# Two-by-two steps for four pairs of up-projection blocks and for one more pair of down-projection rows, in a one-core transformer block

## The chip, the cores and the metric

The kernel runs on one core of a Trainium2 chip. The metric is the device time of one launch in microseconds (us), taken as the median over runs. The core has five engines, each with its own list of instructions that it works through in order: TensorE (PE, matmuls, with weight loads shown apart as PEld), VectorE (DVE), ScalarE (ACT), GpSimd (POOL) and SyncE (SP). SP and POOL also issue most of the transfers (DMAs), from a hardware queue (q1 in the profile, issued by SP) and a software queue (q0, issued by POOL). POOL's DMAs can add to what lies at the destination; the kernel uses them to add weights up in DRAM.

## The reference

One layer of a gated block, batch 1, 512 tokens, width 1024, in float32:

```
h = rms_norm(x);  proj = h @ w_in          # conv B | C | in | q | k | v | f | gates
y_conv = (B * causal_dwconv(C * in)) @ w_out_conv
y_attn = attention(q, k, v, log sigmoid f) @ w_out_attn
x = x + (sigmoid(g_conv) * y_conv + sigmoid(g_attn) * y_attn) @ w_o
h = rms_norm(x)
up = causal_dwconv(h @ w_up)               # 1024 -> 2 * 2816, three taps a channel
a, b = split(up)
x = x + (silu(a) * b) @ w_down             # 2816 -> 1024
return rms_norm(x)
```

The change touches `h @ w_up`, `@ w_down` and what lies between and behind them.

## The kernel before

Activations lie with channels on the 128 partitions and the 512 tokens in the free dimension. Every matmul is 128x128 by 128x256. To keep float32 accuracy each operand is split into a high and a low part of a shorter format; a product is then three matmuls: high by high, low weight by high, high weight by low (`mm3` and `passes`, matmuls of L277 and L295).

**The weights' way.** `stream` lists all weight chunks in the order of use (512 KB for a block of 128 output channels). `load` (L201) brings a chunk to one of five `raw` buffers by an SP DMA; `split` (L244, L248) makes the high part on ACT (`wh_...`) and the low part on DVE (`wl_...`), in two buffers each, so the split of chunk k waits until the matmuls of chunk k-2 are done, and the load of chunk k for the split of chunk k-5. A chunk's matmuls take all products by `wh` first where `passes` orders them so, then those by `wl`. Work that may wait (`later`) is handed out behind the splits.

**Two by two steps.** Where a pair of output blocks by a pair of input blocks is needed, the kernel can do a 2x2 step with 7 products instead of 8 (table `PROD`): each product is of a sum of weights by a sum of activations, and the results are combined afterwards. `double(n)` puts two chunks in the stream for such a step: `P{n}` (768 columns, three plain products, `wst`) and `F{n}` (1024 columns, the four sums of weights). The sums are made in DRAM: `group` yields six operations for each group of two steps, three SP copies (L131) and three adding POOL DMAs (L134), each of which needs the one before; they are issued one at a time by `tick()`, in lockstep for three groups. Ticks come once for a unit of the attention and once for some chunks' splits.

**The stages**, with their time in the profile: attention with the input projections (to about 182 us); the gates, six pairs as 2x2 steps of 84 matmuls, with the mixing products (182 to 295); `wo`, eight blocks (295 to 338), whose evacuation makes x1 = x + p, its scaled high and low parts x1h and x1l, and its squares; the up blocks of phase 0, pairs j = 0 to 11 of two blocks (a and b) of 48 matmuls each (338 to 471); down, phase 0, 12 steps of 42 matmuls (L295 `dn`, 471 to 528); up, phase 1, ten pairs (to 637); down, phase 1, five steps of 42 matmuls for rows 0, 1, 4, 5 of the output (to 660); rows 2 and 3 plainly (`pd`, 120 matmuls, to 674); rows 6 and 7 plainly in two halves of the tokens (`pdA`, `pdB`); then the final norm, the products by it (L1204) and the stores.

**A pair of up blocks.** `up` (L976) multiplies each result by the norm's row (`fz`, from PSUM into SBUF), then takes three taps (L569 on ACT, L570 and L573 on DVE). `glu` makes silu(a) times b (L986 on ACT, L989 and L996 on POOL) and, after every second pair, the sums of the products for the 2x2 steps of down (L1006 to L1011) and their high and low parts (L1015 on ACT, L1016 on DVE).

**The end of down.** `combine` (L1042 to L1061) recombines a finished pair of rows, `final_square` (L1073 to L1078) adds its squares to `ssq3` and scales it. `fin_sum` (L1185 to L1188) and `fin_col` (L1193) do rows 6 and 7; `pc_n` (L336) sums the squares over the partitions on PE and releases the final products and stores of a half of the tokens.

A scheduler (Tile) orders the instructions on each engine by data and priorities, save those that `keep` pins.

Of the kernel before, what the change touches and what calls it, by code (L numbers as in the profile page):

```python
# [59 lines left out]
def block_kernel(ctx, tc, xT, vecs, wv, win, wmix, wo, wup, wst, wdp, outT):  # L60
# [57 lines left out]
    groups += [list(range(n, min(n + 2, NFF))) for n in range(0, NFF, 2)]  # L118
    todo = []

    def group(i):
# [6 lines left out]
        w, f = ((lambda a, b, z=z: z[:, :, a * P : b * P]) for z in (w, t))  # L128
# [16 lines left out]
    for i0, i1 in ((0, ngate), (ngate, len(groups))):  # L145
        for i in range(i0, i1, 3):
            todo += [op for ops in zip(*(group(x) for x in range(i, min(i + 3, i1)))) for op in ops]
# [5 lines left out]
    def double(n):  # L153
        return [(f"P{n}", wst[n, :, : 6 * P], 6 * P), (f"F{n}", sums[n], D)]
# [15 lines left out]
    for ph, (j0, j1) in enumerate(PHASES):  # L170
        stream += [(f"up{j}", wup[j], D) for j in range(2 * j0, 2 * j1)]
        for _ in STEPS[ph]:
            stream += double(n)
            n += 1
# [48 lines left out]
    def split(hl=None):  # L223
# [6 lines left out]
        if k >= gs0 and (nm[0] in "imwu" or nm[0] == "F" and int(nm[1:]) % 2):  # L230
            tick()
        if hl is None:
# [21 lines left out]
        run_later(k, {"u": 1.7, "P": 1.6, "F": 0.75}.get(nm[0], 3.5))  # L254
# [53 lines left out]
    def place_of(f, s_):  # L308
        c = 2 * (f % 3 if f < 6 else 3) + s_
# [140 lines left out]
    for kb in range(KB):  # L450
# [345 lines left out]
    def mt(name):  # L796
        return mp.tile([P, S], F32, tag="mt", name=name, bufs=5)
# [89 lines left out]
    x1 = xp.tile([P, KB, S], F32, tag="x1", name="x1")  # L887
# [50 lines left out]
    for j in range(KB):  # L938
# [3 lines left out]
        xr = mt(f"xr{j}")  # L942
        nc.gpsimd.dma_start(xr, xT[:, j, :])
        nc.vector.tensor_add(x1[:, j, :], p, xr)
        nc.scalar.activation(x1h[:, j, :], x1[:, j, :], AF.Copy, scale=col(G2 + j))
# [381 lines left out]
```

## Time and profile before

| what | value |
|---|---|
| median of 3 runs | 701.1 us (700.32 to 701.42) |
| the profiled execution's time | 700.69 us |
| its span | 698.9 us |
| around the span | 1.8 us |
| PE busy | 690.2 us (99%) |
| DVE, ACT, POOL busy | 498.3 (71%), 341.8 (49%), 156.4 (22%) us |
| granted clock of TensorE, mean | 0.996 |
| moved by DMA | 115.31 MB, mean 165 GB/s |

A row of groups names the line and engine, the operation with what it writes and reads, the count, the busy time and the mean of one in ns, then the idle time ahead of it and who ended it. A matmul's own duration overlaps its neighbours' (a row has 276 ns, but 504 of them take 57.12 us), so the time of a run of matmuls is read from the chain of waits, where a run of matmuls stands as one piece with its start, its length and its count.

### The profile page before, as it was taken

What the parts mean: (1) busy time and instruction counts of PE and PEld (TensorE: products, weight loads), DVE (VectorE), ACT (ScalarE), POOL (GpSimd) and SP (SyncE); (2) the same over time, 40 slices, a digit from 0 to 9 for tenths busy, and PEclk for the clock granted to TensorE, in tenths of its full rate; (3) what the DMA queues carried; (4) which work ended last, traced back from release to release, by engine and by line L of the source; (5) the groups of instructions that cost most, each with busy time, mean ns of one, the idle gap of its engine ahead of it and who ended that gap; (6) DMA issues with size and microseconds to landing.
All of it is one profiled execution on the core that took longest, in us unless ns stands there. A gap on an engine that the chain in (4) does not pass through costs nothing.

```text
span 698.9 us, 14573 instructions
## 1 busy us (share of the span) xinstructions
PE 690.2 (99%) x6005; PEld 688.1 (98%) x6005; DVE 498.3 (71%) x797; ACT 341.8 (49%) x541; POOL 156.4 (22%) x176
## 2 busy tenths in 40 slices
PE   9999999999999999999999999999999999999996
PEld 8999999999999999999999999999999999999995
DVE  6677777786687787754377777778774677877853
ACT  6665656655664433543345443455443345444542
POOL 5125645434011001035321212230000211100002
PEclk9999999999999999999999999999999999999998
DMA  8627877467379777658556637577675433224503
GB/s 308 201 74 209 200 158 200 118 163 179 92 176 268 232 212 214 225 183 207 140 133 197 170 106 199 141 171 206 191 222 177 116 118 92 84 84 133 177 1 121
DMA packets 51538, 115.31 MB, mean 165 GB/s; under 512 B 4720, under 2 KB 22256, under 8 KB 51472
## 3 DMA queue, kind: packets, MB, share of 16 engines
q1 hardware_dynamic: 36880, 93.73, 41.4%
q0 software_dynamic: 13328, 19.44, 17.5%
q10 hardware_dynamic: 1264, 1.22, 0.5%
q8 instruction: 47, 0.77, 0.4%
q14 instruction: 19, 0.16, 0.1%
HBM read 112.20 MB, written 32.51 MB: 207 GB/s over the span
## 4 chain that ended last, share of the span: by engine, by line
PE 92%; DVE 2%; ACT 2%; issue 1%; DMA 1%; ACTq 0%; SPq 0%; POOL 0%; DVEq 0%
PE p_up L277 26%; PE p_in L277 14%; PE dn L295 12%; PE p_up L295 8%; PE gs L295 8%; PE p_wo L277 6%; PE yc L295 3%; PE ya L277 3%; PE pd L277 2%; PE o L659 2%; PE pa L478 2%; PE pb L480 1%; PE tp L644 1%; PE pdB L277 1%; PE pdA L277 1%
## 5 line engine op out<-in xcount | busy, mean ns | idle before, releaser
L277 PE MATMUL p_up<-x1h,wh_up 128*128 128x256 f32 x536 | 104.5, 276 | 0.0
L277 PE MATMUL p_up<-x1l,wh_up 128*128 128x256 f32 x536 | 104.4, 276 | 0.0
L277 PE MATMUL p_up<-x1h,wl_up 128*128 128x256 f32 x536 | 104.3, 276 | 0.0
L244 ACT ACTIVATE wh_up<-raw_up 128x1024 fp32r<-128x1024 f32 x44 | 46.7, 1061 | 89.2 <-PE p_up L277 75.7
L277 PEld LDWEIGHTS p_up<-x1h,wh_up 128*128 128x128 f32 x536 | 80.8, 188 | 0.0
L277 PEld LDWEIGHTS p_up<-x1l,wh_up 128*128 128x128 f32 x536 | 80.7, 188 | 0.0
L277 PEld LDWEIGHTS p_up<-x1h,wl_up 128*128 128x128 f32 x536 | 80.6, 188 | 0.0
L134 POOL DMA_DIRECT2D sum<-in_wst_dram x45 | 47.1, 1122 | 116.4 <-DMA sum<-sum 88.8
L248 DVE TENSOR_TENSOR wl_up<-raw_up,wh_up 128x1024 fp32r<-128x1024 f32 x44 | 53.8, 1223 | 20.8 <-ACT wh_up L244 20.8
L244 ACT ACTIVATE wh_F<-raw_F 128x1024 fp32r<-128x1024 f32 x29 | 30.8, 1063 | 54.6 <-PE ya L277 25.9
L277 PE MATMUL p_in<-xgh,wh_in 128*128 128x256 f32 x288 | 56.8, 279 | 0.0
L277 PE MATMUL p_in<-xgh,wl_in 128*128 128x256 f32 x288 | 56.6, 278 | 0.1
L277 PE MATMUL p_in<-xgl,wh_in 128*128 128x256 f32 x288 | 56.5, 277 | 0.0
L976 DVE TENSOR_TENSOR fz<-p_up,rb_n 128x512 f32<-128x512 f32 x44 | 30.3, 690 | 31.3 <-PE p_up L277 31.3
L248 DVE TENSOR_TENSOR wl_F<-raw_F,wh_F 128x1024 fp32r<-128x1024 f32 x29 | 35.5, 1223 | 17.5 <-ACT wh_F L244 17.5
L277 PEld LDWEIGHTS p_in<-xgh,wh_in 128*128 128x128 f32 x288 | 44.7, 188 | 0.7
L989 POOL TENSOR_TENSOR ge<-fu,fu 128x512 f32<-128x512 f32 x11 | 17.1, 1551 | 120.3 <-DVE fu L573 107.5
L277 PEld LDWEIGHTS p_in<-xgh,wl_in 128*128 128x128 f32 x288 | 43.6, 188 | 0.3 <-DVE wl_in L248 0.3
L277 PEld LDWEIGHTS p_in<-xgl,wh_in 128*128 128x128 f32 x288 | 43.6, 188 | 0.0
L295 PE MATMUL p_up<-x1h,wh_up 128*128 128x256 f32 x168 | 40.3, 277 | 0.0
L295 PE MATMUL p_up<-x1l,wh_up 128*128 128x256 f32 x168 | 40.2, 276 | 0.0
L244 ACT ACTIVATE wh_P<-raw_P 128x768 fp32r<-128x768 f32 x29 | 24.4, 842 | 26.1 <-PE dn L295 14.1
(307 smaller groups left out, 2044.5 us busy)
## 6 DMA issues: line engine op xcount, KB each, us to landing
raw_up<-in_wup_dram SPq DMA_DIRECT2D x44, 512.0 KB, 4.3
raw_F<-sum SPq DMA_DIRECT2D x29, 512.0 KB, 4.6
raw_in<-in_win_dram SPq DMA_DIRECT2D x24, 512.0 KB, 4.5
raw_P<-in_wst_dram SPq DMA_DIRECT2D x29, 384.0 KB, 3.5
sum<-in_wst_dram POOLq DMA_DIRECT2D x29, 256.0 KB, 5.6
sum<-in_wst_dram SPq DMA_DIRECT2D x14, 512.0 KB, 5.6
sum<-in_wst_dram POOLq DMA_DIRECT2D x14, 512.0 KB, 7.3
sum<-sum SPq DMA_DIRECT2D x28, 256.0 KB, 5.9
```

What stands on the lines that cost most here:

```text
L134: return lambda: keep(nc.gpsimd.dma_start(dst, src, accum_op=ALU.add))
L244: ins = nc.scalar.activation(hi, raw, AF.Copy)
L248: ins = nc.vector.tensor_sub(lo, raw, hi.bitcast(F32))
L277: keep(nc.tensor.matmul(out[:, cs], w, x[:, cs], start=start and i == 0 and c == 0, stop=stop and i == 2 and c == len(cut) - 1,))
L295: keep(nc.tensor.matmul(out, wl if x == 1 else wh, xl if x == 2 else xh, start=opens and bk not in seen, stop=closes and bk not in left,))
L478: keep(nc.tensor.matmul(pa[t][:, :VW], xt, w[:, :VW], start=start, stop=stop))
L480: keep(nc.tensor.matmul(pb[t], xt, w[:, VW:], start=start and t % 2 == 0, stop=stop and t % 2 == 1))
L644: keep(nc.tensor.transpose(tp[:, ks], pt[:, ks], ident))
L659: keep(nc.tensor.matmul(o[:, os_], vv[:, kb, pr, e, :], x[:, kb, cs], start=e == 0 and kb == 0 and i == 0, stop=e == 1 and kb == nk - 1 an ...
L976: nc.vector.tensor_mul(z, p, rb2)
L989: keep(nc.gpsimd.tensor_mul(ge, a.rearrange(halves_of, h=2), b.rearrange(halves_of, h=2)))
```

## The change

`UPS = (1, 4, 7, 10)` names four of the twelve pairs of phase 0. For each, `up_pair` does both blocks in two 2x2 steps: 84 matmuls in four chunks (P, F, P, F) into four PSUM banks (`us`), where the pair had 96 in two chunks. The matmuls by sums of activations need sums of the scaled x1 (`tfh`, `tfl`, 16 rows of 128x256 each, in `xf`, the buffer that held the first norm's `xgh`, `xgl`); they are formed while `wo` runs, from a scaled copy `xs2`. To make room, x1 itself goes to DRAM (`x1d`, eight POOL DMAs of 128x512) and comes back after pair 10 (two POOL DMAs) into the same buffer as `xg`, whose second half then serves as scratch for `combine` and for `fz` of phase 1.

The results are recombined in place: a copy on ACT, three 128x256 sums, two 128x512 sums in PSUM. In phase 0 `fz` is no buffer any more: the product by the norm is written back to PSUM, and the taps read it there. The weights' sums for these eight steps are four more groups. Groups now run in lockstep of four, with an extra tick at every second unit of the attention and two for each `u` chunk.

Down, phase 1: rows 2 and 3 go as 2x2 steps too (two full and a half step, 105 matmuls for the 120 of `pd`); only rows 6 and 7 stay plain. `dp` chunks are three instead of six; PSUM banks at the end are named anew; `rs` is copied behind the first final product, and the final products are pinned.

PE has 5909 matmuls instead of 5972 (4 times 12 fewer in up, 15 fewer in down), DVE 855 instructions instead of 799, ACT 552 for 524, POOL 209 for 181, SP 248 for 219.

```diff
 STEPS = (
...
-    (((2, 6), (2, 7)), ((2, 8), (2, 9)), ((0, 6), (0, 7)), ((0, 8), (2, 10)), ((0, 9), (0, 10))),
+    (
+        ((2, 6), (2, 7)), ((2, 8), (2, 9)), ((0, 6), (0, 7)), ((2, 10), (0, 8)), ((0, 9), (0, 10)),
+        ((1, 6), (1, 7)), ((1, 8), (1, 9)), ((1, 10),),
+    ),
...
+UPS = (1, 4, 7, 10)
+NUP = NFF + 2 * (8 - GS)
-PLAIN = [(m, k) for m in (2, 3, 6, 7) for k in range(*PHASES[1])]
-PCUTS = (0, 8, 16, 20, 28, 32, 40)
+PLAIN = [(m, k) for m in (6, 7) for k in range(*PHASES[1])]
+PCUTS = (0, 4, 12, 20)
...
-        for i in range(i0, i1, 3):
+    for i0, i1 in ((0, ngate), (ngate, nup), (nup, len(groups))):
+        for i in range(i0, i1, 4):
...
-    run_later(k, {"u": 1.7, "P": 1.6, "F": 0.75}.get(nm[0], 3.5))
+    run_later(k, 0.45 if nm[0] in "PF" and int(nm[1:]) >= NUP else {"u": 1.7, "P": 1.6, "F": 0.75, "d": 0}.get(nm[0], 3.5))
...
-        nc.vector.tensor_add(x1[:, j, :], p, xr)
+        nc.vector.tensor_add(y, p, y)
...
+        nc.gpsimd.dma_start(x1d[:, j, :], y)
+        nc.scalar.activation(xs2[:, 2 * i : 2 * i + 2].rearrange("p h c -> p (h c)"), y, AF.Copy, scale=col(G2 + j))
+        if i:
+            t1, t3, t4, t2 = b11, b12, b21, b22 = [xs2[:, a] for a in range(4)]
+            nc.vector.tensor_sub(t1, b11, b12)
+            nc.vector.tensor_sub(t3, b22, b12)
+            nc.vector.scalar_tensor_tensor(t2, t1, -1.0, b22, op0=ALU.mult, op1=ALU.subtract)
+            nc.vector.scalar_tensor_tensor(t4, t2, -1.0, b21, op0=ALU.mult, op1=ALU.subtract)
+            qs = slice(4 * q, 4 * q + 4)
+            nc.scalar.activation(tfh[:, qs], xs2, AF.Copy)
+            nc.vector.tensor_sub(tfl[:, qs], xs2, xff[:, qs])
...
+    def up_pair(j):
+        p23, p45, p16, p7 = banks = [acc(f"us{j}{i}") for i in range(4)]
+        pair(up_n(j), x1_form, banks)
...
+            nc.scalar.activation(z[:, lo], p16[:, lo], AF.Copy)
+            nc.vector.tensor_add(z[:, hi], p16[:, hi], z[:, lo])
+            nc.vector.tensor_add(u, p7[:, lo], z[:, hi])
+            nc.vector.tensor_add(z[:, hi], p45[:, hi], z[:, hi])
+            nc.vector.tensor_add(p23, p23, z)
+            nc.vector.tensor_add(p45h, p45h, u.unsqueeze(1).to_broadcast([P, 2, S // 2]))
+        if j == UPS[-1]:
+            xg = xfp.tile([P, 4 * KB, 2 * P], F32, tag="xf", name="xg")
+            for a in range(0, KB, 4):
+                nc.gpsimd.dma_start(x1[:, a : a + 4, :], x1d[:, a : a + 4, :])
...
-            z = fp.tile([P, S], F32, tag="fz", name=f"fz{j}{s_}", bufs=2)
-            nc.vector.tensor_mul(z, p, rb2)
+            z = p if j < PHASES[1][0] else fz(f"fz{j}{s_}")
+            if s_ and j in UPS:
+                nc.vector.scalar_tensor_tensor(z, p, -1.0, rb2, op0=ALU.mult, op1=ALU.mult)
+            else:
+                nc.vector.tensor_mul(z, p, rb2)
```

Three places in the engines' lists. In the rows below, a line number is that of the version that the rows are from.

**VectorE where the up blocks of phase 0 end.** `wl_up23` is the low part of the last up block's weights, `wl_P0` that of the first chunk of down. Before:

```order
L248 TENSOR_TENSOR wl_up23_6058<-raw_up23_5788,wh_up23_6057 128x1024
L570 SCALAR_TENSOR_TENSOR fu101_5981<-fz101_5979,vec_64,fu101_5981 128x511
L1016 TENSOR_TENSOR gl_4521<-go4_5855,gh_4520 128x512
L573 SCALAR_TENSOR_TENSOR fu101_5981<-fz101_5979,vec_64,fu101_5981 128x510
L1016 TENSOR_TENSOR gl_4521<-go4_5855,gh_4520 128x512
L976 TENSOR_TENSOR fz110_6048<-p_up22_5999,rb_n2_4649 128x512
L248 TENSOR_TENSOR wl_P0_6125<-raw_P0_5857,wh_P0_6124 128x768
L570 SCALAR_TENSOR_TENSOR fu110_6050<-fz110_6048,vec_64,fu110_6050 128x511
L573 SCALAR_TENSOR_TENSOR fu110_6050<-fz110_6048,vec_64,fu110_6050 128x510
L976 TENSOR_TENSOR fz111_6114<-p_up23_6065,rb_n2_4649 128x512
L248 TENSOR_TENSOR wl_F0_6153<-raw_F0_5919,wh_F0_6152 128x1024
```

With the change, from `wl_up23` to the two products by the norm (`us100`, `us101`: the results of the stepped pair 10):

```order
L268 TENSOR_TENSOR wl_up23_6153<-raw_up23_5973,wh_up23_6152 128x1024
L1034 TENSOR_TENSOR uz10_6070<-us102_5947,uz10_6070 128x256
L1097 TENSOR_TENSOR gl_4588<-ge4_5804,gh_4587 128x256
L1035 TENSOR_TENSOR uu10_6071<-us103_5948,uz10_6070 128x256
L1097 TENSOR_TENSOR gl_4588<-go4_5943,gh_4587 128x512
L1036 TENSOR_TENSOR uz10_6070<-us101_5946,uz10_6070 128x256
L1097 TENSOR_TENSOR gl_4588<-go4_5943,gh_4587 128x512
L1037 TENSOR_TENSOR us100_5945<-us100_5945,uz10_6070 128x512
L1039 TENSOR_TENSOR us101_5946<-us101_5946,uu10_6071 128x512
L1057 TENSOR_TENSOR us100_5945<-us100_5945,rb_n2_4718 128x512
L1055 SCALAR_TENSOR_TENSOR us101_5946<-us101_5946,rb_n2_4718 128x512
```

and on from there to `wl_P0`:

```order
L1057 TENSOR_TENSOR p_up22_6094<-p_up22_6094,rb_n2_4718 128x512
L594 SCALAR_TENSOR_TENSOR fu100_6082<-us100_5945,vec_64,fu100_6082 128x511
L594 SCALAR_TENSOR_TENSOR fu101_6087<-us101_5946,vec_64,fu101_6087 128x511
L597 SCALAR_TENSOR_TENSOR fu100_6082<-us100_5945,vec_64,fu100_6082 128x510
L597 SCALAR_TENSOR_TENSOR fu101_6087<-us101_5946,vec_64,fu101_6087 128x510
L594 SCALAR_TENSOR_TENSOR fu110_6144<-p_up22_6094,vec_64,fu110_6144 128x511
L1097 TENSOR_TENSOR gl_4588<-go4_5943,gh_4587 128x512
L597 SCALAR_TENSOR_TENSOR fu110_6144<-p_up22_6094,vec_64,fu110_6144 128x510
L1057 TENSOR_TENSOR p_up23_6160<-p_up23_6160,rb_n2_4718 128x512
L268 TENSOR_TENSOR wl_P0_6223<-raw_P0_6003,wh_P0_6222 128x768
L594 SCALAR_TENSOR_TENSOR fu111_6210<-p_up23_6160,vec_64,fu111_6210 128x511
L268 TENSOR_TENSOR wl_F0_6251<-raw_F0_6027,wh_F0_6250 128x1024
```

Between `wl_up23` and `wl_P0` there stood five rows; now there are nineteen, among them the whole recombination and taps of pair 10, and the product of block 23 itself, which stood behind `wl_P0` and waits for block 23's last matmul.

**VectorE at the end, ahead of the first sum of squares** (`ms_n30` reads what `pc_n30` has summed). Before, from one of the last splits of the kernel:

```order
L248 TENSOR_TENSOR wl_dp3_8598<-raw_dp3_8397,wh_dp3_8597 128x1024
L1077 TENSOR_TENSOR ssq3_4522<-ssq3_4522,sq3_2_8601 128x512
L1167 TENSOR_TENSOR x1_4014<-pd3_8521,x1_4014 128x512
L248 TENSOR_TENSOR wl_dp5_8613<-raw_dp5_8490,wh_dp5_8612 128x1024
L1077 TENSOR_TENSOR ssq3_4522<-ssq3_4522,sq3_3_8605 128x512
L1185 TENSOR_TENSOR x1_4014<-pdA_8616,x1_4014 128x256 x2
L1193 TENSOR_TENSOR ssq3_4522<-ssq3_4522,sq3_00_8681 128x256
L341 TENSOR_SCALAR ms_n30_8709<-pc_n30_8704 128x2
```

With the change (`dn112` to `dn115` are the banks of rows 2 and 3):

```order
L1158 TENSOR_TENSOR ssq3_4589<-ssq3_4589,sq3_1_8683 128x512
L1131 TENSOR_TENSOR xg_6078<-dn115_8519,xg_6078 128x256
L1132 TENSOR_TENSOR xg_6078<-dn113_8517,xg_6078 128x256
L1135 TENSOR_TENSOR xg_6078<-xg_6078,dn113_8517 128x512
L1138 TENSOR_TENSOR xg_6078<-xg_6078 128x512
L1142 TENSOR_TENSOR xg_6078<-xg_6078 128x512
L1257 TENSOR_TENSOR xg_6078<-pdA_8703,xg_6078 128x256
L1158 TENSOR_TENSOR ssq3_4589<-ssq3_4589,sq3_2_8695 128x512
L1257 TENSOR_TENSOR xg_6078<-pdA_8703,xg_6078 128x256
L1158 TENSOR_TENSOR ssq3_4589<-ssq3_4589,sq3_3_8699 128x512
L1265 TENSOR_TENSOR ssq3_4589<-ssq3_4589,sq3_00_8768 128x256
L361 TENSOR_SCALAR ms_n30_8796<-pc_n30_8791 128x2
```

The combination of the last pair of down rows and its two square sums now stand directly ahead of `ssq3`'s last sum; before, the two plain chunks of rows 6 and 7 and one square sum stood there.

**SyncE's DMAs in the up stage.** Before:

```order
L201 DMA raw_up14_5190<-in_wup_dram 128x1024
L131 DMA sum9_93<-sum9_93 256x256
L201 DMA raw_up15_5256<-in_wup_dram 128x1024
L131 DMA sum10_94<-sum10_94 256x256
L201 DMA raw_up16_5325<-in_wup_dram 128x1024
L131 DMA sum11_95<-sum11_95 256x256
L201 DMA raw_up17_5387<-in_wup_dram 128x1024
L201 DMA raw_up18_5456<-in_wup_dram 128x1024
L201 DMA raw_up19_5522<-in_wup_dram 128x1024
```

With the change, about pair 7 (chunks P36 to F37), where `sum14`, `sum15` stand for groups of down's weights:

```order
L219 DMA raw_F36_5333<-sum8_92 128x1024
L219 DMA raw_P37_5406<-in_wst_dram 128x768
L219 DMA raw_F37_5468<-sum8_92 128x1024
L140 DMA sum14_98<-sum14_98 256x256
L140 DMA sum15_99<-sum15_99 256x256
L219 DMA raw_up16_5541<-in_wup_dram 128x1024
L219 DMA raw_up17_5565<-in_wup_dram 128x1024
L219 DMA raw_up18_5595<-in_wup_dram 128x1024
L219 DMA raw_up19_5619<-in_wup_dram 128x1024
L140 DMA sum16_100<-sum16_100 256x256
```

Two copies for the sums now stand next to each other ahead of `raw_up16`; before, a load stood between every two of these.

More of the change, by code (lines that the diff above doesn't have):

```diff
@@ L117, in block_kernel @@
     ngate = len(groups)
-    groups += [list(range(n, min(n + 2, NFF))) for n in range(0, NFF, 2)]
+    groups += [[NUP + 2 * j, NUP + 2 * j + 1] for j in range(len(UPS))]
+    nup = len(groups)
+    groups += [list(range(n, min(n + 2, NFF - 1))) for n in range(0, NFF - 1, 2)] + [[NFF - 1]]
+    nstep = [len(d) for d in STEPS[0] + STEPS[1]] + [2] * (2 * (KB - GS) + 2 * len(UPS))
     todo = []
@@ L153, in double, with up_n @@
     def double(n):
-        return [(f"P{n}", wst[n, :, : 6 * P], 6 * P), (f"F{n}", sums[n], D)]
+        h = nstep[n]
+        return [(f"P{n}", wst[n, :, : 3 * h * P], 3 * h * P), (f"F{n}", sums[n][:, : 4 * h * P], 4 * h * P)]
+    def up_n(j):
+        return [NUP + 2 * UPS.index(j) + d for d in range(2)]
     def gate_n(j):
@@ L963, in block_kernel @@
     halves_of = "p (h c) -> p h c"
-    acc = ring(*range(6))
+    acc = ring(4, 5, 6, 7, 0, 1, 2, 3)
     ssq3 = xp.tile([P, S], F32, tag="ssq", name="ssq3")
@@ L1286, in _layout @@
                 win[20 + 8 * m + j][:, (2 * q + k) * P : (2 * q + k + 1) * P]
+                for m, k in order for q in (2 * d, 2 * d + 1)
+            ]
+            wst.append(np.concatenate(w, axis=1))
+    for j in UPS:
+        for d in range(2):
+            w = [
+                wup[2 * j + m][:, (2 * q + k) * P : (2 * q + k + 1) * P]
                 for m, k in order for q in (2 * d, 2 * d + 1)
```

111 lines of the change are left out of this document (71 added, 40 removed).

## The prediction

> **What bounds the kernel now.** First the page's busy times and its chain by engine, then the waits of PE.
>
> ```profile
> PE 690.2 (99%) x6005; PEld 688.1 (98%) x6005; DVE 498.3 (71%) x797; ACT 341.8 (49%) x541; POOL 156.4 (22%) x176
> ...
> PE 92%; DVE 2%; ACT 2%; issue 1%; DMA 1%; ACTq 0%; SPq 0%; POOL 0%; DVEq 0%
> ```
>
> ```profile
> PE warm L103 <- DVE ones L95: 1.0, 1, 1.0
> PE pa L478 <- ACT wh_v L244: 0.6, 1, 0.6
> PE pc_n L336 <- ACT sq L1187: 0.3, 1, 0.3
> ```
>
> PE is busy for 690.2 of 698.9 us, and its waits come to about 2 us, of which the change touches only the 0.3 us ahead of `pc_n` at the end. So the kernel is bound by the number of matmuls: each one left out is worth its issue interval, and each new wait of PE costs its full length. The interval comes from the chain of waits, since a matmul's own row (276 ns) overlaps its neighbours':
>
> ```profile
> 219.85 9.52 PE gs L295 x84
> ...
> 459.79 1.36 PE p_up L295 x12
> 461.15 4.08 PE p_up L277 x36
> ...
> 470.67 57.12 PE dn L295 x504
> ...
> 636.59 23.80 PE dn L295 x210
> 660.39 13.60 PE pd L277 x120
> 673.99 6.80 PE pdA L277 x60
> ```
>
> 57.12 us for 504 is 0.1133 us each; 84 take 9.52, 36 take 4.08: no gap in any stage that the change touches. A block of 48 takes 5.44, a pair 10.88, a stepped pair, like the gates', 9.52.
>
> **The change part by part.** *Matmuls.* 48 fewer in up and 15 fewer in down: 63 x 0.1133 = -7.1 us. All of it lies on the path. The rest is the question of what is late for PE once a pair lasts 9.52 us and its evacuation is longer.
>
> *VectorE in the up stage.* Spacing from start to start, from the groups by form of the up stage and a stretch of VectorE's timeline:
>
> ```profile
> L573 DVE SCALAR_TENSOR_TENSOR fu<-fz,vec,fu 128x510 f32<-128x510 f32 x20 | 14.9, 746 | 0.2
> ...
> L976 DVE TENSOR_TENSOR fz<-p_up,rb_n 128x512 f32<-128x512 f32 x21 | 14.5, 690 | 13.2 <-PE p_up L277 13.2
> L1016 DVE TENSOR_TENSOR gl<-go,gh 128x512 fp32r<-128x512 f32 x15 | 10.3, 684 | 0.0
> ```
>
> ```profile
> 455.52 0.68 DVE L976 TENSOR_TENSOR fz<-p_up,rb_n 128x512 f32<-128x512 f32 x1
> 456.12 1.21 DVE L248 TENSOR_TENSOR wl_up<-raw_up,wh_up 128x1024 fp32r<-128x1024 f32 x1
> 457.26 0.74 DVE L570 SCALAR_TENSOR_TENSOR fu<-fz,vec,fu 128x511 f32<-128x511 f32 x1
> 457.92 0.42 DVE L1016 TENSOR_TENSOR gl<-ge,gh 128x256 fp32r<-128x256 f32 x1
> 458.25 0.74 DVE L573 SCALAR_TENSOR_TENSOR fu<-fz,vec,fu 128x510 f32<-128x510 f32 x1
> ...
> 460.92 1.23 DVE L248 TENSOR_TENSOR wl_up<-raw_up,wh_up 128x1024 fp32r<-128x1024 f32 x1 [0.40 <-ACT wh_up L244]
> ...
> 466.14 0.96 DVE L248 TENSOR_TENSOR wl_P<-raw_P,wh_P 128x768 fp32r<-128x768 f32 x1 [0.19 <-ACT wh_P L244]
> 467.02 0.74 DVE L570 SCALAR_TENSOR_TENSOR fu<-fz,vec,fu 128x511 f32<-128x511 f32 x1
> ```
>
> So a 1024-column split takes 1.14 us of the engine, one of 768 0.88, a product or sum of 512 0.60, a tap 0.66, 256 columns 0.33. A plain pair costs VectorE two splits (2.28), two products (1.20), four taps (2.64) and half of the glu work of two pairs (eight rows, 3.5, so 1.75): 7.9 of 10.88 us. A stepped pair has four splits (4.04) and the recombination (3 x 0.33 + 2 x 0.60 = 2.2) besides: 11.8 of 9.52 us. A stepped and two plain pairs make 27.6 of 31.28 us: VectorE has the time, but falls behind by 2.3 us in a stepped pair, and the next split in its list comes late. Where it comes after PE's need, PE waits.
>
> How early a split can start behind a stepped pair shows in the gates, after the block of 84 that ends at 229.37:
>
> ```profile
> L244 ACT ACTIVATE wh_up<-raw_up 128x1024 fp32r<-128x1024 f32 x44 | 46.7, 1061 | 89.2 <-PE p_up L277 75.7
> ```
>
> ```profile
> 228.50 0.85 ACT L244 ACTIVATE wh_P<-raw_P 128x768 fp32r<-128x768 f32 x1 [1.38 <-PE gs L295]
> ```
>
> ```profile
> 229.46 0.96 DVE L248 TENSOR_TENSOR wl_P<-raw_P,wh_P 128x768 fp32r<-128x768 f32 x1 [1.09 <-PE gs L295]
> ```
>
> ACT's high part starts 0.87 us ahead of the end (the last third of the chunk's matmuls read only `wl`), VectorE's low part 0.09 behind it. Clock 0 be the start of pair 10. F39 ends at 9.52; `wh_up23` (1024, 1.06 long as in the mean of its rows) runs from 8.65 to 9.71, `wl_up23` from 9.75 to 10.89. Then stand 19 rows ahead of `wl_P0`: four of 256 (1.32), eight of 512 (4.80), seven of two operations (4.62), 10.74 in all, to 21.63; `wl_P0`, 0.96, ends at 22.59. PE ends block 23 at 9.52 + 10.88 = 20.40 and reads `wl_P0` after 12 matmuls, at 21.76: it waits **0.8 us**. Before, `wl_P0` stood ahead of block 23's product and was done at 467.10, while PE was still at block 23. Pair 4: 17 rows (four of 256, seven of 512, six of two operations: 9.48) from 10.89 to 20.37; `wl_up12` is done at 21.6, needed after 8 matmuls of the next block at 21.31: **0.3 us**. Behind pairs 1 and 7 fewer rows stand ahead of the next split (the glu rows lie behind it): no wait.
>
> The trace has no tap that reads PSUM. The nearest rows by shape are the taps (0.66) and, for the source, the products from PSUM (690 ns) beside `gl` from SBUF (684 ns): 6 ns apart, so I take 0.66; from above I bound it by the next longer row, 0.88, from below by a plain product, 0.60. That is 11 taps x +0.22 = +2.4 or x -0.06 = -0.7.
> [...]
>
> *ACT* has 49% and gains 28 instructions of under 1 us over 700 us; its copies stand where it waits for PE now. No cost.
>
> *The stage of `wo`.* The squares' sum on POOL must end before `pc_n2`.
>
> ```profile
> L134 POOL DMA_DIRECT2D sum<-in_wst_dram x45 | 47.1, 1122 | 116.4 <-DMA sum<-sum 88.8
> ...
> L989 POOL TENSOR_TENSOR ge<-fu,fu 128x512 f32<-128x512 f32 x11 | 17.1, 1551 | 120.3 <-DVE fu L573 107.5
> ```
>
> ```profile
> 340.48 1.86 POOL L900 TENSOR_TENSOR ssq<-ssq,sq 128x512 f32<-128x512 f32 x1 [3.58 <-ACT sq L899]
> ```
>
> It waits 3.58 us for its square, so the x1 stores, about 1 us each as the issues of L134 are (47.1 us for 45), go into idle time. No cost. The reload of x1 has the rest of up and the first steps of down to land.
>
> *The end.* Before, 13.6 us of plain work hid the combination of the last stepped rows. Now rows 6 and 7 follow at once.
>
> ```profile
> 662.05 0.61 ACT L1076 ACTIVATE sq<-x 128x512 f32<-128x512 f32 x1
> 662.58 1.32 ACT L1078 ACTIVATE x<-x,vec 128x512 f32<-128x512 f32 x2
> 663.80 0.36 ACT L1042 ACTIVATE cz<-dn 128x256 f32<-128x256 f32 x1
> ...
> 682.49 0.84 PE pc_n L336 x8
> ```
>
> Clock 0 be the end of F19. `wl_dp2` needs F19's buffer and runs from 0.7 to 1.8. Behind it stand the end of one combination, the whole of the next, two sums for `pdA` and the squares: eleven rows to the last of row 3's combination, eight of 0.60 and three of 0.33, to 7.6. ACT's square of row 3 (0.53) ends at 8.3, two scalings (0.61 each) at 9.5, the squares of rows 6 and 7 (0.35 each) at 10.2, and `pc_n` can start at 10.3. PE gets there after 75 matmuls, at 8.5 (as 673.99 to 682.49 now): it waits 1.8 instead of 0.3, **+1.5**. The matmuls behind do not fill this, they are pinned.
>
> *Transfers.* A stepped pair loads 1.79 MB (two chunks each of 384 and 512 KB) for 1.05, and its sums are made earlier in the attention, where PE is served from the same lists. What I see for the up stage and the gates:
>
> ```profile
> 220.00:235.00 15.00, 15.00 (x135) 15.00 (x134) 11.54 (x16) 7.00 (x10) 2.04 (x2) 1.00 1.03 268
> 384.00:406.00 22.00, 22.00 (x196) 22.00 (x195) 16.76 (x25) 10.19 (x15) 4.97 (x4) 1.00 0.60 163
> ```
>
> The gates run stepped pairs with DMA engines at a share of 1.03 and 268 GB/s and PE full in 15.00 of 15.00 us, the up stage now at 0.60 and 163. I take no cost, at granted clock 1.00 in both.
>
> *Sum.* -7.1 + 0.8 + 0.3 + 1.5 = -4.5 us. The profiled execution, 700.69 (span 698.9 and 1.8 around it), would be 696.2; it lies 0.4 below the median of 701.1, so on the median **696.6**.
>
> **The rivals.** *B, the waits aren't there* (the rows in between run closer, or the end's chain overlaps): -7.1 to -6.0, 694.0 to 695.1. For it: 28.7% of VectorE is idle. Against it: the lists are fixed, and the spacing above is already gapless. Chance 0.10.
>
> *D, VectorE is dearer.* If the split behind a stepped pair starts as behind a plain block (459.79 to 460.92: 1.13 behind its end), the three waits are 1.2, 1.7 and, at the end, 2.1 more than before: -2.1, or 699.0; with taps at 0.88 as well +0.3, or 701.4. Middle 700.2, no change within what a measurement of this kernel can tell, 0.2% or 1.4 us. Against it: the gates' rows. Chance 0.16.
>
> *C, slower: SyncE is held.* The copies of `sum14` and `sum15` stand next to each other ahead of `raw_up16`, and each waits for an adding POOL DMA. That of `sum14` stands on POOL behind the product of pairs 4 and 5.
>
> ```profile
> raw_up<-in_wup_dram SPq DMA_DIRECT2D x44, 512.0 KB, 4.3
> ...
> sum<-in_wst_dram POOLq DMA_DIRECT2D x14, 512.0 KB, 7.3
> ```
>
> ```profile
> raw_mix<-in_wmix_dram SPq DMA_DIRECT2D x6, 512.0 KB, 7.5
> ```
>
> From pair 4's start: taps done near 20, product 1.6 (L989, 1551 ns), issue 1, so the add starts at 23.0, lands 7.3 later, at 30.3; the two copies take 1.3 to issue, `raw_up16` starts at 31.6 and lands at 35.9; its split is needed near 39.4, after pairs 4 to 7 (40.8 less its own 1.4): 3.5 spare. Ahead of `raw_up22` the same gives 3.1. What hangs on landing is 7.3 + 4.3 = 11.6 us at each place, so landings longer by a factor f cost 2 x 11.6 (f - 1) - 6.6: nothing up to f = 1.27, the whole gain at 1.48, and at 1.6 +7.3, net +2.8: **703.9**. It decides for slower than the bound from f = 1.54. For it: 512 KB loads in the gates took 7.5 us, 1.7 times the median. Against it: in 384 to 406 the share is 0.60, and both terms would have to stretch. Chance 0.18.
>
> That the change does not do what it says is no rival: the 63 matmuls are gone from PE's list.
>
> **How the numbers follow.** Forecast 0.56, B 0.10, D 0.16, C 0.18. The forecast's own range is 695.0 (taps at 0.60, a wait gone) to 699.0 (taps at 0.88). The range of 694.5 to 702.0 takes in D and most of B and leaves out C's far half. Faster: forecast and B, 0.66; same: D, 0.16; slower: C, 0.18.
>
> **What would show it.** In the profile after: a stepped pair is a piece `us` x84 of 9.52 us; PE waits for `wl_P` by 0.8 and for `wl_up` by 0.3 in all, and for the squares ahead of `pc_n` by 1.8. The taps from PSUM have rows near 746 ns. Wrong: waits of PE for `wl_up` behind every stepped pair (D), waits behind which a DMA stands, `raw_up` landing late at pairs 8 and 11 (C), gaps inside the attention, or a `pc_n` wait that is gone.

## The result, and the profile after

| | before | changed |
|---|---|---|
| median of 4 runs | 701.14 us (700.32 to 701.42) | 712.22 us (708.80 to 714.56) |
| ratio, 95% interval | 1 | 1.0156 (1.0121 to 1.0190) |
| profiled execution, its span | 700.69, 698.9 us | 714.36, 712.3 us |

The changed kernel is slower by 1.6%, where 0.6% faster was forecast. Its four runs lie further apart than those of before: 714.4 (the profiled one) and 714.6 us at a mean granted clock of 0.99, 708.8 and 710.1 us at 0.997.

First the changed kernel's page, busy times:

```profile
PE 691.4 (97%) x5942; PEld 687.2 (96%) x5942; DVE 538.7 (76%) x853; ACT 359.0 (50%) x569; POOL 181.1 (25%) x204
```

63 matmuls fewer, and PE is busy for 1.2 us more: PE ran slower somewhere, besides waiting. Its waits (us in total, times, longest) are no longer 2 us but some 14:

```profile
PE p_up L297 <- DVE xr L970: 2.5, 1, 2.5
PE pc_n L356 <- DVE ssq L1265: 2.0, 1, 2.0
PE p_up L315 <- ACT wh_up L264: 1.8, 1, 1.8
PE dn L315 <- DVE wl_P L268: 1.7, 1, 1.7
PE p_up L315 <- DVE wl_up L268: 1.6, 2, 1.1
PE us L315 <- ACT wh_F L264: 1.1, 1, 1.1
...
PE tp L668 <- DVE m L651: 0.6, 1, 0.6
...
PE pc_n L356 <- ACT sq L1259: 0.3, 1, 0.3
```

By stage, from the first matmul of each in PE's timeline (us):

| stage | before | changed | difference |
|---|---|---|---|
| to the first mixing product `yc` (attention, projections) | 182.07 | 185.14 | +3.07 |
| gates | 112.41 | 112.41 | 0 |
| `wo`, to the first up block | 43.52 | 46.17 | +2.65 |
| first 42 matmuls of up and the norm's sum | 5.58 | 7.28 | +1.70 |
| rest of up, phase 0 (48 matmuls fewer, -5.44) | 126.92 | 128.44 | +1.52 |
| down, phase 0 | 57.12 | 59.11 | +1.99 |
| up, phase 1 | 108.80 | 108.80 | 0 |
| down, phase 1, with `pd` (15 fewer) | 37.40 | 35.70 | -1.70 |
| from `pdA` to the end | 25.06 | 29.22 | +4.16 |
| sum | 698.9 | 712.3 | +13.4 |

The 7.1 us of matmuls are saved. 20.5 us come back in six rows of the table (in the rest of up it is 1.52 + 5.44 = 6.96); the forecast had 2.6 of new waits, at three places.

**Between `wo` and up.** PE's timeline at the first up block (a row has its start, its length and the instruction, in brackets the wait ahead of it and who ended it), and windows of 3 to 4 us there (the busy times of PE, PEld, DVE, ACT and POOL, then the granted clock, the share of the DMA engines and GB/s):

```profile
340.85 0.39 PE L297 MATMUL p_wo<-ml,wh_wo 128*128 128x256 f32 x2
343.72 0.47 PE L297 MATMUL p_up<-x1h,wh_up 128*128 128x256 f32 x2 [2.48 <-DVE xr L970]
...
344.49 0.57 PE L297 MATMUL p_up<-x1h,wh_up 128*128 128x256 f32 x2
344.86 0.63 PE L297 MATMUL p_up<-x1h,wl_up 128*128 128x256 f32 x2
```

```profile
341.00:344.00 3.00, 0.52 (x5) 0.35 (x4) 2.87 (x4) 1.99 (x4) 1.68 (x2) 1.00 0.76 216
344.00:348.00 4.00, 4.00 (x23) 4.00 (x22) 3.80 (x5) 1.47 (x3) 4.00 (x6) 0.57 0.78 219
348.00:351.00 3.00, 3.00 (x30) 3.00 (x28) 1.30 (x2) 1.06 (x1) 2.00 (x2) 1.00 1.11 178
```

The first up block has bank 4, the bank of the last `wo` block, so it waits 2.48 us for that block's evacuation on VectorE. Then 16 matmuls go at 0.213 us instead of 0.1133, at a granted clock of 0.57: another 1.6 us, which stands in no list of waits.

VectorE is late there for rows that last too long. Its groups of the `wo` stage, and one of them beside POOL (the two timelines are of the same 4 us):

```profile
L983 DVE TENSOR_TENSOR xs<-xs 128x256 f32<-128x256 f32 x4 | 4.7, 1170 | 0.4
L984 DVE TENSOR_TENSOR xs<-xs 128x256 f32<-128x256 f32 x3 | 4.3, 1423 | 0.4
...
L985 DVE SCALAR_TENSOR_TENSOR xs<-xs 128x256 f32<-128x256 f32 x3 | 1.3, 425 | 0.1
```

```profile
330.13 1.58 POOL L926 TENSOR_TENSOR ssq<-ssq,sq 128x512 f32<-128x512 f32 x1 [0.52 <-ACT sq L925]
```

```profile
330.68 1.31 DVE L983 TENSOR_TENSOR xs<-xs 128x256 f32<-128x256 f32 x1
331.91 0.68 DVE L970 TENSOR_TENSOR xr<-p_wo,xr 128x512 f32<-128x512 f32 x1
```

This difference of 256 columns lasts until 0.28 us after POOL's sum is done, at 331.71. Of the eight such differences of L983 and L984 seven have a POOL sum beside them and take 1.28 to 1.67 us; the first, at 308.86, has none and takes 0.42. POOL's sum of squares comes due at the same point of each block as VectorE's difference.

**In the up stage.** The splits behind stepped pairs are late, as forecast, but by more. VectorE's last rows ahead of pair 6, and POOL at that moment:

```profile
400.43 1.22 DVE L268 TENSOR_TENSOR wl_up<-raw_up,wh_up 128x1024 fp32r<-128x1024 f32 x1
...
407.69 1.40 DVE L594 SCALAR_TENSOR_TENSOR fu<-us,vec,fu 128x511 f32<-128x511 f32 x2
...
410.97 1.95 DVE L268 TENSOR_TENSOR wl_up<-raw_up,wh_up 128x1024 fp32r<-128x1024 f32 x1
```

```profile
410.55 1.30 POOL L1070 TENSOR_TENSOR ge<-fu,fu 128x512 f32<-128x512 f32 x1 [12.69 <-ACT fu L1067]
411.78 2.14 POOL L143 DMA_DIRECT2D sum<-in_wst_dram  x2
...
418.35 2.13 POOL L143 DMA_DIRECT2D sum<-in_wst_dram  x2
```

`wl_up11` starts at 400.43, 0.48 us behind the pair's end at 399.95 (0.09 was taken), since the four sums of the glu work stand ahead of it; the taps from PSUM have the spacing of before (0.66); then `wl_up12` takes 1.95 instead of 1.22 beside POOL's product. Behind pair 7 something else is late, SyncE and the load:

```profile
419.56 4.64 SPq L140 DMA_DIRECT2D sum<-sum  x2
424.30 3.18 SPq L219 DMA_DIRECT2D raw_up<-in_wup_dram  x4
```

```profile
433.47 1.06 ACT L264 ACTIVATE wh_up<-raw_up 128x1024 fp32r<-128x1024 f32 x1 [5.28 <-DMA raw_up<-in_wup_dram]
```

SyncE stood from 413.4, behind `raw_F37`. Its two copies left at 419.56 and 423.70, each within 0.02 us of the landing of the adding DMA that it needs; POOL had issued these two behind its product, at 411.78 and 412.36, and they took 7.8 and 11.3 us to land. `raw_up16` left at 424.30, landed 9 us after its issue, and PE waits 2.0 us. Over this part of the up stage (395 to 470) the landings are slow as a rule; the last figure is the median in us from issue to landing:

```profile
raw_up<-in_wup_dram SPq DMA_DIRECT2D x7, 512.0 KB, 10.3
sum<-in_wst_dram POOLq DMA_DIRECT2D x4, 512.0 KB, 10.7
```

Before, the two had 4.3 and 7.3. This is rival C at one of its two places: both landings were longer, by more than the factor of 1.48 at which its sum has the whole gain gone (21.0 us together for 11.6). `raw_up16` was there 43.3 us behind the start of pair 4 instead of 35.9, which is 3.9 over the spare; PE, itself 1.8 late by then, waited for the rest.

**At the end** PE waits 2.0 us for `ssq3`, close to the 1.8 forecast, and then the clock falls again:

```profile
690.00:694.00 4.00, 1.99 (x19) 1.82 (x17) 3.21 (x7) 3.65 (x8) 0.00 (x0) 1.00 0.00 0
694.00:698.00 4.00, 4.00 (x29) 4.00 (x29) 0.78 (x3) 0.22 (x1) 0.71 (x1) 0.76 0.00 0
```

Two theories for these places. L: VectorE and what it stands behind makes PE wait, each place by itself. M: the time is lost to transfers or to one late engine, and a wait removed comes back at the next place.

### The profile page after: what moved, and what is told of

Its sections match the earlier page's. It is cut to its first block, busy times and chain, and to the rows that moved or that the text cites. A ratio compares the mean times of both kernels' runs of the same rounds, so it can differ in the third digit from the quotient of the medians.

```text
span 712.3 us, 14686 instructions
## 1 busy us (share of the span) xinstructions
PE 691.4 (97%) x5942; PEld 687.2 (96%) x5942; DVE 538.7 (76%) x853; ACT 359.0 (50%) x569; POOL 181.1 (25%) x204
## 3 DMA queue, kind: packets, MB, share of 16 engines
q10 hardware_dynamic: 1264, 1.22, 0.5%
## 5 line engine op out<-in xcount | busy, mean ns | idle before, releaser
L297 PE MATMUL p_in<-xf,wh_in 128*128 128x256 f32 x576 | 95.7, 278 | 0.0
L297 PE MATMUL p_up<-x1l,wh_up 128*128 128x256 f32 x440 | 86.2, 277 | 0.0
L297 PEld LDWEIGHTS p_in<-xf,wh_in 128*128 128x128 f32 x576 | 80.4, 188 | 0.7
L264 ACT ACTIVATE wh_F<-raw_F 128x1024 fp32r<-128x1024 f32 (+1 forms) x40 | 42.0, 1051 | 64.4 <-PE ya L297 25.9
L268 DVE TENSOR_TENSOR wl_F<-raw_F,wh_F 128x1024 fp32r<-128x1024 f32 (+1 forms) x40 | 49.3, 1231 | 24.9 <-ACT wh_F L264 24.6
L297 PE MATMUL p_in<-xf,wl_in 128*128 128x256 f32 x288 | 56.6, 278 | 0.1
L268 DVE TENSOR_TENSOR wl_P<-raw_P,wh_P 128x768 fp32r<-128x768 f32 (+1 forms) x40 | 37.8, 944 | 14.2 <-ACT wh_P L264 8.6
L297 PEld LDWEIGHTS p_in<-xf,wl_in 128*128 128x128 f32 x288 | 43.5, 188 | 0.3 <-DVE wl_in L268 0.3
L315 PE MATMUL dn<-gl,wh_F 128*128 128x256 f32 x156 | 36.4, 276 | 0.0
L315 PE MATMUL dn<-gh,wh_F 128*128 128x256 f32 x156 | 36.3, 276 | 0.0
## 6 DMA issues: line engine op xcount, KB each, us to landing
sum<-in_wst_dram POOLq DMA_DIRECT2D x19, 512.0 KB, 10.1
```

The lines of the kernel that those rows point to most:

```text
L264: ins = nc.scalar.activation(hi, raw, AF.Copy)
L268: ins = nc.vector.tensor_sub(lo, raw, hi.bitcast(F32))
L297: keep(nc.tensor.matmul(out[:, cs], w, x[:, cs], start=start and i == 0 and c == 0, stop=stop and i == 2 and c == len(cut) - 1,))
L315: keep(nc.tensor.matmul(out, wl if x == 1 else wh, xl if x == 2 else xh, start=opens and bk not in seen, stop=closes and bk not in left,))
```

## The experiments

All are edits of the changed kernel unless said otherwise, against the kernel before run beside them (700.9 to 701.0 us); the ratios are to that kernel. Since the changed kernel's own runs spread over 5.8 us, what one edit is worth is read from the stage times of the profiles.

**The banks of `wo`**

```diff
+    acc = ring(5, 6, 0, 1, 4, 2, 7, 3)
     po = None
     for j in range(KB):
```

> The changed kernel with one edit: the blocks of wo take their PSUM banks in the order 5, 6, 0, 1, 4, 2, 7, 3 instead of 5, 6, 0, 1, 2, 7, 3, 4, so that the first up block (bank 4) no longer needs the evacuation of the last wo block. Theory L (PE waits where VectorE is late, each place by itself, and a wait of 2 us or more is followed by some 4 us of matmuls at half rate): the wait of 2.5 us ahead of up0 goes, PE then waits some 1.1 us for the sum of squares ahead of pc_n2, and the 16 slow matmuls (1.6 us) go: -3.0 us. Rival M (the lost time is transfers or another late engine, and a wait removed comes back at the next place): within 0.5 us of the changed kernel, with the wait ahead of pc_n2 or in the first stepped pair grown by as much.

711.80 us, ratio 1.0148 (1.0133 to 1.0163). The wait ahead of up0 is gone (`wo` takes 43.52 again), 0.9 came back ahead of `pc_n2` as expected, and the half-rate matmuls did not go: 16 of them came behind that wait, at 348.8. From `wo`'s start to the first stepped pair it is 59.0 instead of 60.5 us: -1.5, half of what L gave. The bank was one cause; VectorE's lateness behind it is another. The half rate comes in some executions only: four other kernels with this stage as in the changed one (next splits ahead, late sum, fewer sums, fill) have the same wait of 2.5 us, no half rate behind it, and take 58.9.

**The sums of squares on VectorE**

```diff
-            nc.gpsimd.tensor_add(ssq, ssq, sq)
+            nc.vector.tensor_add(ssq, ssq, sq)
```

> The changed kernel with one edit: the seven sums of squares of the wo stage (L926) run on VectorE instead of POOL. [...]

710.03 us, 1.0131 (1.0116 to 1.0146). Two readings of the long differences were open: that they are long by themselves, and that they last so long beside POOL's sum. The groups of the `wo` stage:

```profile
L926 DVE TENSOR_TENSOR ssq<-ssq,sq 128x512 f32<-128x512 f32 x7 | 4.8, 685 | 0.0
...
L983 DVE TENSOR_TENSOR xs<-xs 128x256 f32<-128x256 f32 x4 | 1.7, 419 | 0.0
L984 DVE TENSOR_TENSOR xs<-xs 128x256 f32<-128x256 f32 x4 | 1.7, 419 | 0.0
```

The same rows in the same place take 419 ns, where rows that are long by themselves would have kept their 1.3 us or more: they were long because POOL's sum ran beside them. From `wo`'s start to the first stepped pair it is 57.3 us, -3.2 (the author's estimate was -3: eight differences 0.9 us shorter, seven sums of 0.6 us more), and the wait ahead of up0 is 0.9. Half of the 3.2 is that wait, which the edit shortened by 1.6; the other half is the half rate, which also stays away in the four profiles with the full wait. Seven sums more on VectorE made it earlier.

**The down part undone**

```diff
-        ((2, 6), (2, 7)), ((2, 8), (2, 9)), ((0, 6), (0, 7)), ((2, 10), (0, 8)), ((0, 9), (0, 10)),
-        ((1, 6), (1, 7)), ((1, 8), (1, 9)), ((1, 10),),
+    (((2, 6), (2, 7)), ((2, 8), (2, 9)), ((0, 6), (0, 7)), ((0, 8), (2, 10)), ((0, 9), (0, 10))),
...
-PLAIN = [(m, k) for m in (6, 7) for k in range(*PHASES[1])]
+PLAIN = [(m, k) for m in (2, 3, 6, 7) for k in range(*PHASES[1])]
...
```

> The changed kernel with the down part of the change undone: phase 1 of down has its five steps again, rows 2 and 3 of the output are done plainly, with the chunks and banks of before; the up part stays. Theory L: 15 matmuls more (+1.7 us), but the plain work covers the last combination again: the wait of 2.0 us ahead of pc_n is 0.3 again, the 13 slow matmuls behind it go (1.3) and the end is as before: -2.5 us net. Rival M: the end was late for what came before it, and the time is +1.7.

710.18 us, 1.0128 (1.0110 to 1.0145). The end from `pdA` on takes 25.5 us instead of 29.2, for 1.7 us more of matmuls: -2.0, near L.

**The next splits ahead of the recombination**

```diff
         pair(up_n(j), x1_form, banks)
+        was = dict(order)
+        ahead[2 * j + 2] = block(f"up{2 * j + 2}", x1h, x1l, True)
+        while len(parts) < chunk.n + 2:
+            split()
+        order.update(was)
...
```

> The changed kernel with one edit in the order of the work: behind a stepped pair the next block's matmuls and the two next splits are put ahead of the pair's recombination and taps, so that wl_up12, wl_up18 and wl_P0 stand seven to nine rows earlier in VectorE's list. Theory L: the waits for wl_up12 (1.2 us), wl_up19 (0.6) and wl_P0 (1.85) go or fall under 0.3 each: -3 us. Rival M (VectorE has too much to do in a stretch of three pairs, or the loads are late): the waits move on to the blocks behind, and the time stays within 0.7 us.

707.98 us, 1.0105 (1.0090 to 1.0120). Up from the first stepped pair to down takes 116.6 instead of 121.4 us: -4.8. (The seven profiles in which nothing was edited in this stage took 119.7 to 121.4, so the gain is 3.1 to 4.8.) The waits for `wl_up12`, `wl_up19` and `wh_up16` are gone; what is left ahead of pair 10 and ahead of down is

```profile
PE dn L315 <- DVE fu L597: 1.0, 1, 1.0
...
PE us L315 <- DVE wl_P L268: 1.0, 1, 1.0
```

L, with more than it gave: in this order POOL issues the adding DMAs ahead of its product, SyncE's two copies left at 406.99 and 411.40, and `raw_up16` left 9 us earlier, counted from the start of pair 4. So this edit moved the transfers too, and its gain is not VectorE's alone.

**The sum of squares at the end behind more matmuls**

```diff
-    plain7(0, 1, kall[:5])
+    plain7(0, 1, kall)
+    sqB = [fin_sum(1, 0)]
+    plain7(1, 1, kall[:1])
     rcA = fin_col(0, sqA)
-    plain7(0, 1, kall[5:])
+    plain7(1, 1, kall[1:6])
     fin_out(0, rcA)
-    sqB = [fin_sum(1, 0)]
-    plain7(1, 1, kall)
+    plain7(1, 1, kall[6:])
```

> The changed kernel with one edit at the end: the first sum of squares over the partitions (pc_n30) comes behind 33 matmuls of pdB instead of 15, and the final products of that half behind 15 more. Theory L: PE fills the time in which VectorE and ACT finish the last combination; the wait of 2.0 us ahead of pc_n30 falls to about 0, the half-rate matmuls behind it (1.3 to 2.8 us in the profiles so far) go: -2 to -4 us. Rival K (the end is a chain of VectorE work, not PE's wait: the last products and stores come as late as before): within 1 us of the changed kernel.

709.79 us, 1.0127 (1.0110 to 1.0144): the end takes 26.9 us instead of 29.2, the first wait and the half-rate matmuls are gone, and 1.3 us of wait has come up ahead of the second sum, behind the products of the first half. L for -2.3, K for the rest.

**Six gate groups in lockstep**

```diff
-        for i in range(i0, i1, 4):
+        w = 4 if i0 else 6
+        for i in range(i0, i1, w):
...
```

> The changed kernel with one edit: the six gate groups of weight sums run in lockstep of six instead of four, so that on POOL's queue more operations lie between a copy and the adding DMA that waits for it. Theory P (in the attention POOL stands still at adding DMAs whose copies have not landed, and the products of the convolution behind them hold ACT and PE): the waits of PE in the attention (0.65 to 1.8 us in the profiles so far) go, POOL's waits for sums in the attention fall: -1 us. Rival Q (these waits come from VectorE or from the clock at the start): no change there.

710.69 us, 1.0138 (1.0111 to 1.0165); the runs lie between 708.4 and 712.8, too far apart for 1 us to show. In the profile the waits of PE for `pp` and `m` in the attention are gone (0.6 us in the changed kernel, 1.4 to 1.8 in the seven others of its kind without this edit), and `yc` starts at 182.50 instead of 185.14; beside the kernel with the old down part, whose start had nearly the same clock, it is 182.50 for 183.67: P, with -1.2 us. All four kernels with this edit start `yc` at 182.1 to 182.8, the eight stepped ones without it at 183.7 to 185.1. The rest of those 2.6 us lies at the start: the matmuls ran at half rate to 10.1 us in the changed kernel's profile, to 4.8 in that of before and to between 4.6 and 6.7 in those of the experiments.

**The down part alone**, on the kernel before (the first two hunks of the diff of `STEPS` and `PLAIN`, with their chunks and banks):

> The kernel before with the down part of the change alone (rows 2 and 3 in 2x2 steps, only rows 6 and 7 plain); the up part, the stay of x1 in DRAM and the extra ticks are left out. Theory L: 15 matmuls fewer (-1.7 us), and the end 4.2 us longer than before, as in the changed kernel (a wait of 2.0 us ahead of pc_n, slow matmuls behind it): +2.5 us against the kernel before, 703.5. Rival M (the end was late only for what the up part left behind): 699.4.

703.37 us, 1.0032 (1.0020 to 1.0043): L's number. The wait is there without the up part:

```profile
PE pc_n L342 <- DVE ssq L1190: 2.1, 1, 2.1
```

Down has the matmuls' gain (35.70 us instead of 37.40), and the end takes 29.2 us. The down part by itself loses 2.4 us.

**Fewer sums**

```diff
-    for i0, i1 in ((0, ngate), (ngate, nup), (nup, len(groups))):
+    for i0, i1 in ((0, ngate), (ngate, nup), (nup, nup + 4)):
...
+        f = sums[n] if n in sums else wst[n]
```

> The changed kernel without the weight sums from sum14 on (all but the first four groups of down; their steps read plain weights instead, so that part of the output is left wrong in value but all matmuls, splits and loads stay). SyncE then has no copies to wait for about pairs 7 and 10. Theory S (SyncE, held by the copies of sum14 and sum15 behind POOL's adding DMAs, starts raw_up16 late, and its load is slow among the others): the wait for wh_up16 (1.4 to 2.3 us in the profiles so far) goes; the waits behind VectorE (wl_up12 1.2, wl_P0 1.7) stay: -1.5 to -2 us. Rival V (wh_up16 is late because ACT and VectorE are behind): all waits of the up stage stay.

707.51 us, 1.0106 (1.0079 to 1.0132). The wait behind pair 7 is gone (the pair takes 9.52, the two behind it 21.76). Those that are left in the up stage and ahead of down:

```profile
PE dn L316 <- DVE wl_P L269: 1.7, 1, 1.7
PE p_up L316 <- DVE wl_up L269: 1.1, 1, 1.1
...
PE us L316 <- ACT wh_F L265: 0.3, 1, 0.3
```

The waits behind VectorE stay: S. From the first stepped pair to down it takes 117.3 us for 121.4, or for the 119.7 to 121.4 of all seven profiles with nothing edited in this stage: -2.5 to -4.1 us, more than the 1.5 to 2 expected. The wait for `wl_up19` went too (1.3 in the two pairs behind pair 7), and that for `wh_F38` fell from 1.1 to 0.3. This kernel also moves fewer bytes, so it does not tell the queue that stands still from slow landings; the kernel with the next splits ahead keeps every transfer, issues them earlier, and has no wait there either.

**16 matmuls more in the gap at the end**

```diff
+    warm_on(16)
     rcA = fin_col(0, sqA)
```

> The changed kernel with 16 more matmuls, whose result nobody reads, ahead of the first sum of squares at the end (pc_n30), where PE waits 2.0 us; nothing else moves. Theory H (a wait of about 2 us is followed by matmuls at half rate): PE is busy in the gap, the half-rate matmuls of pdB behind it (1.3 to 2.8 us lost in the profiles so far) go, and the end is shorter by as much although work was added. Rival I (those matmuls are slow for another reason, such as the loads or the last stores): they stay, and the time is the same or up to 0.5 us longer.

709.99 us, 1.0135 (1.0117 to 1.0154). The windows of the end:

```profile
686.00:690.40 4.40, 4.38 (x38) 4.17 (x36) 3.96 (x8) 3.31 (x7) 0.00 (x0) 1.00 0.00 0
690.40:694.00 3.60, 3.53 (x31) 3.56 (x31) 0.74 (x3) 0.57 (x2) 0.71 (x1) 1.00 0.00 0
```

The clock stays at 1.00 behind the gap, the 30 last matmuls take 3.52 us (4.51 in the changed kernel), and the end takes 27.6 us; the ends of the seven profiles with the open gap, the changed kernel's among them, took 29.2 to 31.3. H: adding work to PE made it shorter by 1.6 us or more.

**Five edits together** (banks, squares, splits, late sum, lockstep):

> The changed kernel with five edits together: the banks of wo in the other order, the sums of squares on VectorE, the splits ahead of the recombination, the late sum of squares at the end, the lockstep of six. Theory L: the gains add up, -1.5 (banks) and -3.2 (squares) overlap at about -3.7, splits -4.2, end -3, lockstep -1: 712.2 - 12 = 700, beside 701 before. Rival M (the waits move on): above 704.

700.01 us, 0.9985 (0.9975 to 0.9994): L's number. Against the median of the changed kernel it is -12.2, between the two profiles -14.8 (712.3 to 697.5), so that the number is met to the tenth is luck; that the gains add up and the waits do not move on is shown. The time is only just below before.

**Three stepped pairs**

```diff
-UPS = (1, 4, 7, 10)
+UPS = (1, 4, 7)
...
-    acc = ring(4, 5, 6, 7, 0, 1, 2, 3)
+    acc = ring(*range(8))
...
```

This kernel has the new banks of up in place of the edit of `wo`'s banks.

> Like the kernel with all five edits, but pair 10 is done plainly (three stepped pairs, 12 matmuls more: +1.4 us) and the banks of up begin at 0, so that neither wo nor the sum of squares meets a bank in use. Theory L: the waits at the end of the up stage go (1.1 ahead of the stepped pair 10, 1.0 ahead of down): -2.1 + 1.4 = -0.7 us, 699.3. Rival M: VectorE is as late there with a plain pair: 701.4.

699.50 us, 0.9983 (0.9973 to 0.9994). The waits ahead of pair 10 and of down are gone, but a new one of 1.8 us stands ahead of `wl_up20`, which VectorE does nine rows behind block 18's product. Both theories have a part.

**Each next split ahead, in plain pairs too**

```diff
                 p = block(f"up{2 * j + s_}", x1h, x1l, True)
+                while j < PHASES[1][0] - 2 and len(parts) < chunk.n + 1 and stream[len(parts)][0][0] == "u":
+                    split()
```

> Like the kernel with three stepped pairs, but in the plain pairs too the next block's split is put ahead of the evacuation of the block before it, so that wl_up20 stands right behind the product of block 18 instead of nine rows later. Theory L: the one wait left in the up stage (1.8 us for wl_up20) goes: -1.8 us, 697.7, and the up stage has no wait of PE over 0.3. Rival M: the rows put behind come late at the next place: within 0.7 us of the kernel with three pairs.

697.53 us, 0.9952 (0.9939 to 0.9966): L. Its waits of PE, all of them:

```profile
PE pc_n L357 <- ACT sq L1274: 1.3, 1, 1.3
PE warm L108 <- DVE ones L100: 1.0, 1, 1.0
PE pa L503 <- ACT wh_v L265: 0.4, 1, 0.4
PE pb_n L371 <- POOL rc_n L364: 0.2, 1, 0.2
```

This beats both kernels, by 0.5% the one before. 51 matmuls fewer are worth 5.8 us; the span is 694.8 for 698.9. The end still takes 26.4 us for 25.1, and the first stepped pairs 0.2 and 0.4 more than 9.52.

## Why the prediction was wrong

The forecast was -4.5 us, the profile has +13.4. The 17.9 between them are 4.35 from `wo` to the norm's sum, 6.66 in the rest of up, 1.19 ahead of down, 2.66 at the end and 3.07 ahead of `yc`.

- *Matmuls, -7.1.* Right: down, phase 1, which waits for nothing, is shorter by just its part (-1.70).
- *"The stage of `wo`... No cost."* This step failed: +2.65 of wait and +1.70 behind it. It looked at POOL's row and asked whether POOL had time; it never priced the rows that the sums of x1 put on VectorE, and did not see that POOL's sum would run beside them. It did not follow the new order of the banks either. The squares' experiment shows the first, the banks' the second; each takes 1.5 to 1.6 us off the wait, and 1.6 of the rest is the half rate, which came in three of seven profiles with this wait.
- *"Transfers... I take no cost."* This step failed by as much. Behind pair 7 PE waited 2.0 us, through the mechanism that rival C gives; with `wl_up19` and `wh_F38` behind it 2.5 to 4.1 us over the up stage, by the kernel with fewer sums. A share of 0.60 over 22 us of the kernel before said nothing about a queue that stands still and then has four loads at once, nor about landings of 10.3 and 10.7 us. In the attention a like queue, POOL's, cost 1.2.
- *VectorE's rows by their spacing.* The terms 0.3 and 0.8 came out as 1.24 and 1.85 us (gaps in PE's timeline over one matmul's interval), by the mechanism named. The rows themselves cost what was taken, taps from PSUM too (0.66); what was not in the sum was POOL beside them (0.7 us on `wl_up12`, 0.7 on a `gl` row ahead of `wl_P0`), and the four glu sums that stand ahead of `wl_up11` and `wl_up23` (0.4 and 0.5). Rival D had these sizes, 1.2 and 1.7, for a cause that was not the one: the splits were held by rows ahead of them and by POOL. Of the stepped pairs only pair 7 took the 9.52 us that were said; pairs 1, 4 and 10 took 10.2, 9.9 and 10.9.
- *The end, +1.5.* The wait was right in its kind and nearly in size (2.0 for 1.8), but the 0.3 that was taken off stands ahead of the second sum, in both kernels, so the term should have been 1.8. The price was +4.16: 2.2 at the first sum, 1.6 in the work behind it at half rate, 0.4 behind the last sum. The prediction held that "each new wait of PE costs its full length". Two of them cost more, since the matmuls behind ran at half rate.
- *Rival C* had the right direction, and its 703.9 is a quarter of the way from before to what was measured. No rival had the time of 712: the forecast looked for one mechanism to decide, and there were several, each of 1 to 4 us, all in one direction.

Chance has a part in the size. In the profiled execution half rate cost some 5 of the 13.4 us: 1.8 at the start of the kernel (18 matmuls more than before), 1.6 behind `wo`, 1.6 at the end. Only the last came in every profile that has its wait.

Left open: why half rate follows one 2.5 us wait and not another (below), and how much of the changed kernel's spread of 5.8 us it makes; only one of its four runs has a profile.

## What to carry to other kernels

Where PE is full, moving work off it pays only while every engine that feeds it keeps its places; count the rows that a change adds on each of them in each stage, not only in the one that it is about. A wait is cheap to remove once it is found in the order of instructions (here splits behind evacuations, an adding DMA behind a product): three of the edits change one to three lines. And check which engine runs beside a row, not only how long the row takes elsewhere.

## What the hardware showed

**Rows of VectorE beside POOL.** A 256-column difference of two SBUF operands took 1.28 to 1.67 us beside POOL's sum of two SBUF operands, 0.42 without it; each of the seven long ones ended 0.28 to 0.30 us behind the end of that sum. With the seven sums on VectorE all eight took 419 ns in the mean. A 1024-column split took 1.95 us beside POOL's product, 1.22 without it. A product by the norm, which reads PSUM and one SBUF operand, took its usual 0.69 us in the midst of a POOL product (386.36 us, POOL from 385.05 to 387.58). There POOL's own row was long: that product took 2.53 us, for 1.30 of the one at 410.55, and two `gl` rows of VectorE with two SBUF operands, 1.28 us together as elsewhere, ran in its first half. Why rows of the two engines take longer beside each other, and whether it hangs on where their operands lie, no run shows. The profile of before has such rows too: 1.65 us for a split of 1024 columns at 53.80 (1.23 at 51.85), 1.07 for a difference of 256 columns at 149.46, 1.33 for a tap at 358.43 (0.74 in the mean of its group); PE has no wait at any of the three.

**PE at half rate behind a wait.** Behind the 2.0 us wait at the end the matmuls ran at half rate in all seven profiles that have the gap; behind the 2.5 us wait between `wo` and up in three of seven; behind pair 7 in two of seven, after waits of 2.3 and 1.5 us; once behind 0.9 us with sums of one column around it; the filled gap had none. Each time 13 to 28 matmuls took 0.213 us, 1.3 to 2.8 us lost in all; in the changed kernel's profile the granted clock was 0.51 over the one such stretch (344.49 to 347.84 us) and 0.50 over the other (696.10 to 699.48). The length of the wait alone does not decide it: in the same profile the matmuls behind 1.82 us (434.58) and behind 1.69 us (482.66) went at 0.11 to 0.12 us each from the second on, and four of the seven waits of 2.5 us have no half rate behind them. What does decide it, no run shows.
